# TensorE in source order, with longer attention steps and reordered joints, in a two-layer attention decoder

## The chip, the core and the metric

The kernel runs on one NeuronCore of a Trainium2 chip. The metric is device time in microseconds, the median of several executions. The engines work side by side, each through its own list of instructions in order: TensorE (PE; its weight loads appear as PEld), VectorE (DVE), ScalarE (ACT), GpSimd (POOL) and SyncE (SP), which issues the transfers. An instruction waits on semaphores for those of other engines.

## The reference

Two decoder layers on 256 tokens of 1024 numbers, all in float32. Layer A is differential attention: 8 heads, each with two q/k maps of 64 and values of 128. Layer B takes one shared K/V of the residual stream and three groups of dilated windows, 16 heads of 64 for each, whose outputs are mixed by their softmax denominators. Each layer ends with an output projection and a squared-ReLU MLP of width 4096, both added to the residual stream.

```python
# layer A
h = rms_norm(x, a_norm)
q, k, v = split(h @ w_qkv)                      # q, k normalized per 64, gained, rotated
p = softmax(mask(q @ k.T / 8))                  # two maps a head
a = p[:, :, 0] - lam * p[:, :, 1]
x = x + (rms_norm(a @ v, sub_gain) * (1 - lam_init)) @ w_o
x = x + square(relu(rms_norm(x) @ w_up)) @ w_down
# layer B
k, v = split(rms_norm(x, kv_norm) @ kv_w)       # k normalized and rotated, 3 groups
q = rms_norm(x, b_norm) @ w_q                   # the same
o = sum over groups of softmax(lse) * attention(q_g, k_g, v_g)
x = x + o @ w_o
x = x + square(relu(rms_norm(x) @ w_up)) @ w_down
```

## The kernel before

Precision comes from pairs of reduced-precision parts: each weight chunk is split into a high part (`whi`, ScalarE, L82) and a remainder (`wlo`, VectorE, L83), activations likewise, and a product takes three matmuls (L292 to L294, L402 to L404, L488 to L490) or two (L435, L437). `Weights` fetches chunks of up to 128 x 2048 on SP's queue in the order of the list that `plan` made, three chunks ahead, and splits them by halves, at most five halves being alive; a half is given back by `release` after its last matmul.

Layer A: for each of 8 heads one gemm of 384 columns (q, k and values of the head) over 8 k-tiles and two token blocks, in four quarters of 12 matmuls (`gemm`, `gemm_half`). Out of its PSUM banks come the values (L675, L676) and, by `qk_rows`, the normalized and rotated q and k: a square on ScalarE, table product, sum and mean on VectorE, then three instructions on GpSimd (L328 rotation sum, L332 power -1/2, L334 scaling).
The attention of a head is a generator, `attn_A`: transposes of q and k and their split (`qk_T`, L357 and L340/L341); scores (L350), masked maxima (`masked`, L369), their scaled negative `nm` (L538), exponentials (L541), the combination of the two maps (L545 to L550); transposes of the probabilities and split (L554, L558); the product with the values (L565, L566) and normalization (L569 to L580); transposes into the projection's input `oTh`/`oTl` (L584 to L591).
`tick` is called after each quarter (in the projection after each token block, 6 matmuls). It lets the weights split up to two halves, and every live generator come one step nearer to its next part: `yield n` means that the next part follows n ticks later. `WAIT_A` and `WAIT_B` hold these numbers. `start` enters a generator, `finish` ticks until it is done.

Layer B: 8 pairs of heads, each with three gemms of 384 columns, q, k and values, 12 quarters together; `attn_B` starts after the values' gemm. It makes three q/k transposes (a group each), scores and masked maxima of query block 0, then of block 1, then the softmax of both (L612 to L623), then for each head of the pair the transposes of the probabilities (L632) and the product with the values (L646) with its addition (L649 to L651) and the split into `oTh`/`oTl` (L652).

`OutProj` runs over 8 k-tiles: six by `body` while the last generators finish, the last two by `group`, one of four (token block, half of the columns) at a time. `Mlp.run` runs over 16 chunks, up product of chunk j before down product of chunk j-1; the last two down products are left to `Mlp.group`. `boundary` closes a projection or MLP: groups and residual additions (L421, L519), transposes of the new x by halves (`make_hT`, L260, L268, L271), and the first products of the next stage (`first`).

PSUM has 8 banks, shared by all accumulators and transposes (tag `bank`). The q/k row tiles have 6 buffers, the values' tiles 3, softmax tiles 2.

The order in which each engine gets its instructions is set, in this kernel, by the tile framework's scheduler: it goes through the program with a cost model and takes on each engine, of the instructions that are ready by the model, the one that is earliest in the source. `high_priority` moves some splits ahead. This holds for TensorE too.

## Time and profile before

| | |
|---|---|
| Median of 3 runs | 801.36 us (800.72 to 801.68) |
| Profiled execution | 801.55 us, its span 799.5 us |
| Instructions | 11766 |
| PE, matmul | 772.1 us busy (97%), 4408 |
| PEld, weight loads | 686.7 us (86%) |
| DVE | 581.1 us (73%), 985 |
| ACT | 467.0 us (58%), 851 |
| POOL | 190.9 us (24%), 191 |
| DMA | 131.12 MB, mean 164 GB/s |
| Granted TensorE clock | 0.995 of full speed in the mean |

The span runs from the first to the last instruction, times in the rows are counted from its start. Layer A's heads run up to about 101 us, its projection to 137, the first MLP to 314, layer B's pairs to 577, their projection to 617, and the second MLP to the end. In the middle of layer A a head takes 12.1 us. Matmuls are pipelined and their modelled ends overlap, so what a matmul takes of TensorE's time is the distance of two starts, and idle time shows where the pipe ran dry. In a list of instructions, the bracket behind one is the engine's idle time before it and what ended it.

### The profile page before, as it was taken

The page shows a single profiled execution, that of the slowest core. Times are in us where ns is not written, and L with a number is a line of the kernel's source. Part 1 is how long each engine was busy: PE and PEld are TensorE (multiplying, and loading weights), DVE is VectorE, ACT ScalarE, POOL GpSimd, SP SyncE. Part 2 cuts the span into 40 slices and gives each one's busy share as a digit, 9 for nine tenths or more (in the row PEclk, how much of TensorE's full clock was granted, in tenths as well). Part 3 has the DMA queues.
Part 4 walks back from the last instruction along what each step waited for, and adds up shares of the span by engine and source line. Part 5 has one row for each costly group of instructions (what it writes and reads, how often), then busy time and mean ns, then how long its engine had stood idle before and what let it go on. Part 6 is the DMA issues. An engine that isn't in the chain of part 4 may idle for free.

```text
span 799.5 us, 11766 instructions
## 1 busy us (share of the span) xinstructions
PE 772.1 (97%) x4408; PEld 686.7 (86%) x4408; DVE 581.1 (73%) x985; ACT 467.0 (58%) x851; POOL 190.9 (24%) x191
## 2 busy tenths in 40 slices
PE   6999989999999999999999999999997999999998
PEld 6898967888888888999999999999886888888886
DVE  3998987666656666998888888888767666556663
ACT  5667777544444445657586674857766544444441
POOL 2553531300000000555336354363611000000000
PEclk9999999999999999999999999999999999999999
DMA  8643445445555542554443434434442455545531
GB/s 300 229 143 123 158 155 164 169 171 197 198 176 207 171 184 90 187 198 154 136 153 113 157 121 157 158 119 172 159 158 106 158 186 182 210 170 199 187 130 52
DMA packets 22328, 131.12 MB, mean 164 GB/s; under 512 B 2560, under 2 KB 3328, under 8 KB 13056
## 3 DMA queue, kind: packets, MB, share of 16 engines
q1 hardware_dynamic: 22272, 130.38, 46.0%
q8 instruction: 34, 0.56, 0.3%
q14 instruction: 22, 0.18, 0.1%
HBM read 129.32 MB, written 1.05 MB: 163 GB/s over the span
## 4 chain that ended last, share of the span: by engine, by line
PE 64%; DVE 17%; ACT 12%; issue 3%; POOL 2%; DMA 1%; SPq 0%; POOLq 0%; DVEq 0%; ACTq 0%
PE wps L435 15%; PE wps L437 7%; PE acc L488 7%; PE acc L489 7%; PE acc L490 7%; DVE wlo L83 5%; PE acc L292 4%; PE acc L294 4%; PE acc L293 4%; ACT whi L82 4%; ACT sm L618 2%; DVE sm L369 2%; PE wps L632 2%; DVE T L317 2%; ACT smA L541 2%
## 5 line engine op out<-in xcount | busy, mean ns | idle before, releaser
L83 DVE TENSOR_TENSOR wlo<-raw,whi 128x1024 fp32r<-128x1024 f32 (+1 forms) x272 | 307.0, 1138 | 153.9 <-ACT whi L82 153.7
L82 ACT ACTIVATE whi<-raw 128x1024 fp32r<-128x1024 f32 (+1 forms) x272 | 258.9, 957 | 211.1 <-issue 74.9
L435 PE MATMUL wps<-hT,whi 128*128 128x512 f32 x512 | 182.2, 399 | 2.0 <-DVE hT L271 2.0
L437 PE MATMUL wps<-hT,wlo 128*128 128x256 f32 x512 | 142.9, 280 | 0.0
L435 PEld LDWEIGHTS wps<-hT,whi 128*128 128x128 f32 x512 | 95.9, 188 | 26.0 <-DVE hT L271 3.2
L328 POOL TENSOR_TENSOR T<-T 128x384 f32<-128x384 f32 (+1 forms) x48 | 44.4, 924 | 280.5 <-DVE ms L243 181.6
L488 PE MATMUL acc<-whi,u 128*128 128x512 f32 x256 | 100.4, 392 | 0.3 <-ACT u L340 0.3
L489 PE MATMUL acc<-wlo,u 128*128 128x512 f32 x256 | 100.0, 391 | 0.0
L490 PE MATMUL acc<-whi,u 128*128 128x512 f32 x256 | 98.9, 389 | 0.0
L437 PEld LDWEIGHTS wps<-hT,wlo 128*128 128x128 f32 x512 | 96.6, 189 | 1.4
L292 PE MATMUL acc<-whi,hT 128*128 128x384 f32 x256 | 88.8, 349 | 0.3 <-ACT whi L82 0.2
L292 PE MATMUL acc<-whi,hK 128*128 128x384 f32 x256 | 87.6, 343 | 0.0
L293 PE MATMUL acc<-wlo,hT 128*128 128x384 f32 x256 | 86.3, 337 | 1.1 <-DVE wlo L83 1.1
L294 PE MATMUL acc<-whi,hT 128*128 128x384 f32 x256 | 86.2, 337 | 0.0
L294 PE MATMUL acc<-whi,hK 128*128 128x384 f32 x256 | 85.8, 335 | 0.0
L293 PE MATMUL acc<-wlo,hK 128*128 128x384 f32 x256 | 85.7, 335 | 0.0
L332 POOL TENSOR_TENSOR f<-ms,half 128x6 f32<-128x6 f32 (+1 forms) x48 | 68.2, 1422 | 4.6 <-DVE ms L323 3.1
L488 PEld LDWEIGHTS acc<-whi,u 128*128 128x128 f32 x256 | 48.1, 188 | 11.7 <-ACT u L340 1.2
L490 PEld LDWEIGHTS acc<-whi,u 128*128 128x128 f32 x256 | 48.1, 188 | 10.6 <-DVE u L341 0.4
L489 PEld LDWEIGHTS acc<-wlo,u 128*128 128x128 f32 x256 | 48.1, 188 | 8.8
L293 PEld LDWEIGHTS acc<-wlo,hT 128*128 128x128 f32 x256 | 48.6, 190 | 1.4 <-DVE wlo L83 1.4
L292 PEld LDWEIGHTS acc<-whi,hT 128*128 128x128 f32 x256 | 48.6, 190 | 1.4 <-ACT whi L82 0.5
(117 smaller groups left out, 1204.9 us busy)
## 6 DMA issues: line engine op xcount, KB each, us to landing
raw<-in_wB SPq DMA_DIRECT2D x48, 768.0 KB, 4.2
raw<-in_wup SPq DMA_DIRECT2D x32, 1024.0 KB, 4.8
raw<-in_wdn SPq DMA_DIRECT2D x32, 1024.0 KB, 4.8
raw<-in_wA SPq DMA_DIRECT2D x15, 768.0 KB, 4.3
raw<-in_woA SPq DMA_DIRECT2D x4, 1024.0 KB, 4.8
raw<-in_woB SPq DMA_DIRECT2D x4, 1024.0 KB, 4.8
early<-in_x SPq DMA_DIRECT2D x2, 512.0 KB, 5.3
x<-in_xp SPq DMA_DIRECT2D x1, 1024.0 KB, 7.5
```

The lines of the kernel that those rows point to most:

```text
L82: self.nc.scalar.activation(hi[:, :n], raw, AF.Copy)
L83: self.nc.vector.tensor_tensor(lo[:, :n], raw, hi[:, :n].bitcast(F32), op=ALU.subtract)
L292: nc.tensor.matmul(ps, h[:, kt, 0, tok], wh[:, c], start=kt == 0, stop=False)
L293: nc.tensor.matmul(ps, h[:, kt, 0, tok], wl[:, c], start=False, stop=False)
L294: nc.tensor.matmul(ps, h[:, kt, 1, tok], wh[:, c], start=False, stop=kt == KT - 1)
L328: nc.gpsimd.tensor_tensor(u[:, :n].rearrange("p (h a d) -> p h a d", a=2, d=HD // 2), T[:, 0, :n].rearrange("p (h a d) -> p h a d", a=2, d ...
L332: nc.gpsimd.tensor_tensor(f[:, :nsub], ms[:, :nsub], half[:, :nsub], op=ALU.pow)
L435: nc.tensor.matmul(o, wh[:, c], self.h[:, kt].rearrange("p l s -> p (l s)"), start=kt == 0, stop=False, skip_group_check=True)
L437: nc.tensor.matmul(o[:, 0:S], wl[:, c], self.h[:, kt, 0, :], start=False, stop=kt == KT - 1, skip_group_check=True)
L488: nc.tensor.matmul(ps, uh[:, tok], dh[:, c], start=first, stop=False)
L489: nc.tensor.matmul(ps, uh[:, tok], dl[:, c], start=False, stop=False)
L490: nc.tensor.matmul(ps, ul[:, tok], dh[:, c], start=False, stop=last)
```

## The change

- TensorE's instructions run in the order of the source; the other engines keep the scheduler.
- The numbers of ticks become (3, 2, 4, 3, 4) in layer A and (4, 2, 2, 5, 3, 3) in layer B, and the last head of A waits three more at its start.
- `masked` gives the scaled negative maximum itself, as a minimum of scaled scores; `nm` is not computed any more, and the exponentials take the scale -1.
- In layer A `cf`'s second half is a square on ScalarE, the mean's factor is in the squares, and the addition `ms` is on GpSimd.
- In layer B each query block has its softmax right behind its scores. A generator starts after k; the order of the gemms is q, k, values for six pairs, then q, k, q, k, values, values.
- The last two heads of layer A: one gemm of 512 columns for q and k of both, in ticks of half a quarter, then one of 256 for the values of both.
- `boundary` ticks after three groups, makes x's first half right behind them, and runs `first` by quarters with the second half's transposes after the first of them. The MLP leaves only its last down product to the groups.

```diff
-WAIT_A = (2, 2, 4, 2, 3)
-WAIT_B = (2, 2, 2, 2, 2, 3)
+WAIT_A = (3, 2, 4, 3, 4)
+WAIT_B = (4, 2, 2, 5, 3, 3)
+PAIRS = [(hp, i) for hp in range(HP - 2) for i in range(3)]
+PAIRS += [(HP - 2 + e, i) for e, i in ((0, 0), (0, 1), (1, 0), (1, 1), (0, 2), (1, 2))]
...
-    def gemm_half(pss, h, key, j, i, n):
+    def gemm_half(pss, h, key, j, i, n, nk=2):
         for t in range(NT):
+            if t and n != 384:
+                tick()
...
+        for g in range(KT // nk):
+            gemm_half(pss, h, key, g // 2, g % 2, n, nk)
+            if g < KT // nk - 1:
+                tick()
...
-        f = small.tile([P, 8], F32, name="f", tag="f")
+        f = small.tile([P, 16], F32, name="f", tag="f")
...
-    def masked(out, ps, m, init, mx):
-        nc.vector.tensor_tensor_reduce(out, ps, m, 1.0, init, ALU.add, ALU.max, mx)
+    def masked(out, ps, m, nm):
+        nc.vector.tensor_tensor_reduce(out, ps, m, -(HD ** -0.5), 3e38, ALU.add, ALU.min, nm)
...
     def boundary(group, add, outs, ssx, first):
-        for t in range(NT):
-            group(t, 0)
-            add(t, 0)
+        for t, n in ((0, 0), (1, 0), (0, 1)):
+            group(t, n)
+            add(t, n)
             tick()
-        group(0, 1)
-        add(0, 1)
         make_hT(x, 0, outs)
         square_sums(ssx, x, 0)
         group(1, 1)
         add(1, 1)
-        first(0)
+        first(0, 0)
         make_hT(x, 1, outs)
         square_sums(ssx, x, 1)
-        first(1)
+        for i, f in ((0, 1), (1, 0), (1, 1)):
+            first(i, f)
...
             for j in range(1, NFC):
                 nu = self.up(j)
-                if j == NFC - 1:
-                    self.tail = [u, nu]
-                    return
...
         def group(self, t, n):
-            for i in range(2):
-                for f in range(2):
-                    self.down_mm(NFC - 2 + i, self.tail[i], f, t, n)
+            for f in range(2):
+                self.down_mm(NFC - 1, self.u, f, t, n)
...
     def attn_A(hd, qr, kr, vt, oh, ol):
-        yield WAIT_A[0]
+        yield WAIT_A[0] + 3 * (hd == KT - 1)
...
-        nc.vector.tensor_scalar(nm, mx, -(HD ** -0.5), None, op0=ALU.mult)
...
-        nc.vector.scalar_tensor_tensor(cf[:, :, 1], den[:, :, 0], EPS, den[:, :, 0], op0=ALU.mult, op1=ALU.mult)
+        nc.scalar.activation(cf[:, :, 1], den[:, :, 0], AF.Square, scale=EPS ** 0.5)
...
-        nc.vector.scalar_tensor_tensor(ms[:, :2], oss, 1.0 / P, cf[:, :, 1], op0=ALU.mult, op1=ALU.add)
+        nc.gpsimd.tensor_tensor(ms[:, :2], oss, cf[:, :, 1], op=ALU.add)
...
     # attn_B, for each query block b, behind its scores
+            for hh in range(2):
+                nc.scalar.activation(sms[hh][:, b, :], sms[hh][:, b, :], AF.Exp, bias=nm[:, hh:hh + 1],
+                                     scale=-1.0, accum_out=den[:, hh:hh + 1])
+            nc.vector.reciprocal(rd, den)
+            for hh in range(2):
+                nc.scalar.activation(sms[hh][:, b, :], sms[hh][:, b, :], AF.Copy, scale=rd[:, hh:hh + 1])
+            yield WAIT_B[2 + b]
...
-    for hd in range(KT):
+    for hd in range(KT - 2):
...
+    pss = gemm(h, ("Aqk",), 512)
+    vt2 = [values_tile() for _ in range(2)]
+    for e in range(2):
+        qns = rows_A(pss, e * 4 * HD)
+        gens.append(start(attn_A(KT - 2 + e, qns, qns, vt2[e], oh, ol)))
+    tick()
+    pss = gemm(h, ("Av",), 256, 4)
+    for e in range(2):
+        values_A(pss, e * P, vt2[e])
+    tick()
...
+    for hp, i in PAIRS:
+        pss = acc0 if hp == 0 and i == 0 else gemm(hx, ("B", hp, i), 384)
...
+        if i == 1:
+            gens.append(start(attn_B(hp, *[[rows[hp, e, t] for t in range(NT)] for e in range(2)], vts[hp],
+                                     oh, ol)))
...
-    with tile.TileContext(nc) as tc:
+    with tile.TileContext(nc) as tc, tc.manual_schedule(engines={mybir.EngineType.PE}):
```

## Rows read from the trace of the kernel before

**Rows 1.** Windows by stage: length, busy us (instructions) by engine, clock, DMA share, GB/s
```profile
60.41:101.50 41.09, 38.22 (x253) 36.24 (x251) 37.35 (x106) 30.75 (x93) 17.38 (x22) 1.00 0.43 151
101.50:137.10 35.60, 31.51 (x161) 24.03 (x161) 28.51 (x73) 26.71 (x76) 7.70 (x10) 0.95 0.40 137
...
577.00:616.70 39.70, 35.68 (x202) 28.79 (x201) 27.56 (x45) 26.73 (x47) 4.87 (x5) 0.96 0.41 148
```

**Rows 2.** Waits of PE: releaser, total us, times, longest us
```profile
PE wps L350 <- DVE tl L341: 4.1, 4, 1.9
PE wps L632 <- ACT sm L623: 3.9, 6, 1.0
...
PE wps L435 <- DVE hT L271: 2.0, 2, 1.5
```

**Rows 3.** Timeline of one head of layer A: start us, us, engine, line
```profile
73.14 0.60 PE L357 MATMUL wps<-ident,qn 128*128 128x128 f32 x4
...
73.84 0.51 ACT L541 ACTIVATE smA<-smA,nm 128x256 f32<-128x256 f32 x1 [2.67 <-DVE nm L538]
...
77.11 0.58 ACT L340 ACTIVATE th<-wps 128x512 fp32r<-128x512 f32 x1
...
79.19 0.38 PE L350 MATMUL wps<-th,tl 64*128 64x256 f32 x2 [0.96 <-DVE tl L341]
```

**Rows 4.** Groups of VectorE by shape, two heads: busy us, mean ns, idle before
```profile
L538 DVE TENSOR_SCALAR nm<-mx 128x4 f32<-128x4 f32 x2 | 0.7, 366 | 0.0
...
L576 DVE SCALAR_TENSOR_TENSOR ms<-oss,cf 128x2 f32<-128x2 f32 x2 | 0.3, 148 | 0.0
```

**Rows 5.** Timeline of one pair of layer B, ScalarE and TensorE
```profile
466.55 0.72 ACT L618 ACTIVATE sm<-sm,nm 128x512 f32<-128x512 f32 x1 [1.83 <-DVE nm L616]
...
470.92 0.33 PE L293 MATMUL acc<-wlo,hK 128*128 128x384 f32 x1
471.09 0.34 PE L294 MATMUL acc<-whi,hK 128*128 128x384 f32 x1
471.99 0.33 PE L632 MATMUL wps<-ident,sm 128*128 128x128 f32 x1 [0.56 <-ACT sm L623]
```

**Rows 6.** Window with the lower granted clock, columns as in rows 1
```profile
105.90:109.30 3.40, 3.32 (x9) 2.64 (x10) 3.40 (x15) 1.31 (x2) 3.14 (x5) 0.51 0.40 166
```

**Rows 7.** Groups of GpSimd by shape, two heads of layer A
```profile
L332 POOL TENSOR_TENSOR f<-ms,half 128x4 f32<-128x4 f32 x4 | 4.0, 1011 | 0.2
L334 POOL TENSOR_TENSOR qn<-T,f 128x256 f32<-128x256 f32 x5 | 3.8, 770 | 0.4
L328 POOL TENSOR_TENSOR T<-T 128x256 f32<-128x256 f32 x4 | 3.0, 738 | 0.2
L578 POOL TENSOR_TENSOR ors<-ms,half 128x2 f32<-128x2 f32 x2 | 1.4, 696 | 11.9 <-DVE ms L576 11.9
```

**Rows 8.** Timeline of TensorE, the last head's end in layer A
```profile
126.65 0.28 PE L566 MATMUL wps<-v,pA 128*128 128x256 f32 x1
...
129.28 0.39 PE L402 MATMUL acc<-whi,oTh 128*128 128x512 f32 x1
129.50 0.39 PE L403 MATMUL acc<-wlo,oTh 128*128 128x512 f32 x1
130.07 0.33 PE L584 MATMUL wps<-ident,orow 128*128 128x128 f32 x1 [0.18 <-ACT orow L580]
```

**Rows 9.** Timeline of TensorE, the last pair's end in layer B
```profile
606.92 1.22 PE L646 MATMUL wps<-p,v 128*128 128x512 f32 x6 [0.94 <-DVE p L341]
...
610.78 0.53 PE L402 MATMUL acc<-whi,oTh 128*128 128x512 f32 x1 [2.65 <-ACT oTh L340]
```

**Rows 10.** Timeline of a boundary's copies on ScalarE and VectorE, and of a residual addition
```profile
135.73 1.55 ACT L268 ACTIVATE hT<-wps,gcol 128x256 fp32r<-128x256 f32 x4
...
136.59 1.66 DVE L271 SCALAR_TENSOR_TENSOR hT<-wps,gcol,hT 128x256 fp32r<-128x256 f32 x4 [0.21 <-ACT hT L268]
...
795.91 0.75 DVE L519 SCALAR_TENSOR_TENSOR x<-acc,rM,x 128x512 f32<-128x512 f32 x1 [1.97 <-PE acc L490]
```

More of the change, by code (lines that the diff above doesn't have):

```diff
@@ L130, in plan_mlp @@
                 plan(("dn", layer, j - 1), a["wdn"][layer, j - 1], 2 * DM)
-    for hd in range(KT):
+    for hd in range(KT - 2):
         for i in range(2):
             plan(("A", hd, i), a["wA"][hd, i], 4 * 384)
+    for i in range(2):
+        plan(("Aqk", i), a["wAqk"][i], 4 * 512)
+    plan(("Av", 0), a["wAv"], 8 * 256)
     for i in range(4):
@@ L137, in trunk @@
     plan_mlp(0)
-    for hp in range(HP):
-        for i in range(3):
-            for j in range(2):
-                plan(("B", hp, i, j), a["wB"][hp, i, j], 4 * 384)
+    for hp, i in PAIRS:
+        for j in range(2):
+            plan(("B", hp, i, j), a["wB"][hp, i, j], 4 * 384)
     for i in range(4):
@@ L295, in gemm_half, with gemm @@
         W.release(at[(*key, j)], i)
-    def gemm(h, key, n):
+    def gemm(h, key, n, nk=2):
         pss = [accum() for _ in range(NT)]
-        for j in range(2):
-            for i in range(2):
-                gemm_half(pss, h, key, j, i, n)
-                if not (j == 1 and i == 1):
-                    tick()
+        for g in range(KT // nk):
+            gemm_half(pss, h, key, g // 2, g % 2, n, nk)
+            if g < KT // nk - 1:
+                tick()
         return pss
@@ L454, in relu2, with first @@
             return uh, ul
-        def first(self, i):
-            if i == 0:
+        def first(self, i, f):
+            if i == 0 and f == 0:
                 self.ps = [wps(), wps()]
-            for f in range(2):
-                self.up_mm(0, f, range(4 * i, 4 * i + 4))
-                if i == 1:
-                    W.release(at[("up", self.layer, 0)], f)
-                    self.pre(f)
-                tick()
+            self.up_mm(0, f, range(4 * i, 4 * i + 4))
             if i == 1:
+                W.release(at[("up", self.layer, 0)], f)
+                self.pre(f)
+            tick()
+            if i == 1 and f == 1:
                 self.u = self.relu2()
@@ L599, in attn_B @@
         yield WAIT_B[1]
-        mxs = [small.tile([P, 2], F32, name="mx", tag="mx") for _ in range(2)]
         sms = [wk.tile([P, 2, 4 * P], F32, name="sm", tag="sm") for _ in range(2)]
@@ L705, in trunk, with first_B @@
     acc0 = []
-    def first_B(i):
-        if i == 0:
+    def first_B(i, j):
+        if i == 0 and j == 0:
             acc0.extend([accum(), accum()])
-        for j in range(2):
-            gemm_half(acc0, hq, ("B", 0, 0), i, j, 384)
-            if not (i == 1 and j == 1):
-                tick()
+        gemm_half(acc0, hq, ("B", 0, 0), i, j, 384)
+        if not (i == 1 and j == 1):
+            tick()
     boundary(mlp.group, mlp.add, [(3, hq), (2, hk)], ssx, first_B)
@@ L718, in trunk @@
     gens = []
[L719 to L736 removed]
+    rows, vts = {}, [[] for _ in range(HP)]
+    for hp, i in PAIRS:
+        hx = hk if i else hq
+        pss = acc0 if hp == 0 and i == 0 else gemm(hx, ("B", hp, i), 384)
+        for t in range(NT):
+            ps = pss[t]
+            if i < 2:
+                rows[hp, i, t] = qk_rows(ps, 2 * G, rb[NT + t], windows(tabB[:, i, t]))
+            else:
+                vt = wk.tile([P, 2 * G, 2, HD], F32R, name="v", tag="v", bufs=3)
+                psv = ps[:, :384].rearrange("p (g d) -> p g d", d=HD)
+                nc.scalar.activation(vt[:, :, 0, :], psv, AF.Copy, scale=rb[t])
+                nc.vector.scalar_tensor_tensor(vt[:, :, 1, :], psv, rb[t], vt[:, :, 0, :].bitcast(F32),
+                                               op0=ALU.mult, op1=ALU.subtract)
+                vts[hp].append(vt)
+        tick()
+        if i == 1:
+            gens.append(start(attn_B(hp, *[[rows[hp, e, t] for t in range(NT)] for e in range(2)], vts[hp],
+                                     oh, ol)))
     op = OutProj("oB", oh, ol)
```

80 lines of the change are left out of this document (30 added, 50 removed).

## The prediction

> **What bounds the kernel now.** First the busy times by stage. In layer A's heads (60.4 to 101.5 us) TensorE is idle for 41.09 - 38.22 = 2.9 us and VectorE is busy for 37.35 of 41.09; from there to the first MLP TensorE is idle for 4.1 us, and from 577.0 to 616.7, where layer B's last pairs run out, for 4.0 [rows 1]. Second, who ended its stops: the low halves `tl` of the transposed q/k (4.1 us), the softmax `sm` (3.9, in layer B's pairs) and `hT` (2.0) [rows 2]. So TensorE is the bound, only its stops can be won, 2.9 + 4.1 + 4.0 + 3.9 or some 15 us, and in layer A VectorE is close behind it. Third, one such stop. A head's q/k transposes start at 73.14 and end at 73.74; ScalarE copies them only at 77.11, because the exponentials of the head before, which had waited 2.67 us for `nm`, stood in its queue; so the scores start at 79.19, after 0.96 us of idle TensorE [rows 3]. The reader is to see that the distance in steps would do if ScalarE's queue were empty.
>
> The sum goes against the profiled execution's 801.55 us (span 799.5 and 2.05 around it); the median of the runs is 801.36, so 0.2 is taken off at the end.
>
> **Layer A's heads.** `nm` now comes out of the masking instruction (scale -1/8, minimum): 0.37 us a head less on VectorE and in the chain. The square in `cf` goes to ScalarE (0.15 us), and the `ms` addition, also 128x2, to GpSimd [rows 4]. VectorE's share falls from 0.91 [rows 1] to about 0.86 at the same pace (0.67 of the 12 us that a head takes). The first map's exponentials no longer wait for the second map's masks and for a weight split between. The q/k transposes come one step later, which gives GpSimd time. Four stops lie in this stretch, 2.9 us of idle, and each costs about 0.17 more, because the pipe refills (a stop with 0.56 us idle stretched a spacing of 0.17 to 0.90 [rows 5]): 3.5 us. VectorE stays close to full, so I leave a quarter: **-2.7** (bounds: -3.5, all gone; +1, `tl` and `qn` late at more heads).
>
> **From layer A to its projection (101.5 to 137.1).** Of the time here 4.1 us are idle, and in 105.9 to 109.3 the granted clock is at its lower level of 1.2 GHz (0.51 [rows 6]); the stretch's mean of 0.95 makes that 0.05 x 35.6 = 1.8 us [rows 1]. It came after a stop of 1.9 us, the longest by `tl` [rows 2].
> The edit computes q and k of the last two heads first (512 wide), then both values (256 wide). Columns and weight bytes stay; four weight chunks become three, one transfer less on SP's queue, and DMA is 0.40 busy [rows 1], so transfers stay hidden (a late chunk would cost its landing of 4 to 5 us once). What changes is where the chains end. GpSimd gets four row preparations at once, each 1.01 + 0.77 + 0.74 = 2.5 us [rows 7]: 10.1 us, and normalizations of earlier heads between. Until the last head's q/k transposes I count 5.6 us of values, two projection steps of 6 products at 0.22 [rows 8] = 2.7, and some 3.5 of other heads' pieces, 11.8 together: a stop of about 0.8 (0 to 4, the upper end by the 3.4 us that a copy lagged in rows 3).
> The last head's output is late too. Before, its transposes came 130.07 - 126.65 = 3.4 us after the start of the last values product, 3.3 after its end [rows 8], and the scheduler had laid some thirteen projection products into that time. Now the values product comes with the eleventh projection step and the transposes after the twelfth and three empty steps; in source order one step (1.4 us) and another head's two transposes (0.2) lie between: a stop of 1.7, with the addition on GpSimd (0 to 0.70, the power of as many elements [rows 7]) 1.9.
> The `tl` stop falls from 1.9 to 0.6. The 1.5 us before the MLP (most of `hT`'s 2.0 [rows 2]) fall to 0.6: no weight half is released before the last group, so no split stands ahead of the copies there. The half clock goes with its stop; I give a new one, after the 1.9, one chance in two. Sum: 0.8 + 1.9 - 1.3 - 0.9 - 1.8 + 0.9 - 0.5 (small stops by output rows) = **-0.9** (bounds -4 and +7).
>
> **Layer B's pairs.** The repeating stop: the maxima of both blocks come first, ScalarE waits 1.83 us for `nm`, and the probability transposes find `sm` unfinished, 471.09 to 471.99 [rows 5]. Six such stops hold 3.9 us of idle [rows 2], 4.8 with the refill. Now the softmax goes block by block without `nm`, with five steps instead of four between the second block's scores and the transposes: 5 x 12 products at 0.17 = 10.4 us, against two exponentials and two scalings of 0.72 each [rows 5] behind two masks, under 5 us. They go. Starting after k instead of v brings the q/k transposes nearer to k: five steps and the pieces between, 13 us, against two row preparations of 2.5 x 1.5 = 3.8 us each (estimate by rows 7, 384 columns for 256). New is one cluster of 26 pieces behind a pair's first step, which wants 9 of 8 PSUM banks: two of the gemm, one kept by the second value tile, 1 + 2 + 3 of the pieces. The output's bank comes free about when the third transposes want it. I take 0.5 in all: **-4.3** (bounds -5.4 and +2).
> The Trainium skill (Perfetto Trace Analysis, Optimization Strategy) says that a gap that repeats on the engine that should be saturated can mean that SBUF or PSUM is short for the next tile. Here the releaser is ScalarE's work on `sm`, not a freed bank, so the trace does not bear it out; by the rule longer steps, which hold tiles longer, would keep the 4.8.
>
> **The last two pairs.** q and k of both come first, then the values, so pair six ends in the fourth projection step and pair seven in the twelfth, the last; before, four empty steps followed. The values product that waited 0.94 us for `p` [rows 9] has three steps instead of two and does not wait. The last output still needs the 2.65 us up to the projection [rows 9], and only three products of the other tile (0.7) now stand in front: 2.0. Around the first projection step more than eight banks are wanted, and pair seven's second softmax tile waits for pair six's transposes: +0.6. The half clock (0.04 x 39.7 = 1.6 us [rows 1]) follows a shorter stop: I take off 0.7. Together -0.9 - 0.2 (refill) - 0.7 + 0.6 - 0.7 = **-1.9** (bounds -4 and +3).
>
> **Boundaries and the end.** The down products of the last chunk but one now run before the boundary, so the last `u` has 24 products (5.4 us) of cover and costs nothing. But a group has 6 products instead of 12: 1.4 us of cover. Into layer B ScalarE's four copies (1.55 us) and VectorE's four (1.66) come twice, and the last addition (0.75) queues behind VectorE's [rows 10], so the second transposes wait about 0.9: **+0.9** (0 to 2.5, if the copies are late at all three boundaries). The final outputs leave at half the spacing: **+0.1**. The wider `f` tile is off every chain: 0.
>
> Sum: -2.7 - 0.9 - 4.3 - 1.9 + 0.9 + 0.1 = -8.8; 801.55 - 8.8 - 0.2 = 792.6, say **793**.
>
> **Rivals.** *The joint of layer A decides, to the slower side.* In source order nothing passes a late instruction. If the copies' lag of 3.4 us [rows 3] stays and four row preparations meet it, the heads' 2.7 are not won, `qn` costs 4, `tl` 1.9 more than before, the output transposes 1.9 + 2, another half-clock stretch 1.8: +11.6 there, -4.3 - 1.9 + 1.0 elsewhere, 801.4 + 6.4 = 808. It decides once the joint costs over 5.2. For it: VectorE at 0.91 [rows 1]; against: no stop by these tiles is longer than 1.9 now [rows 2].
> *All ends are hidden.* The lighter VectorE runs ahead, and bank waits, boundary and half clock cost nothing: 793 - 0.8 - 1.3 - 0.9 - 0.5 - 0.9 - 0.6 = 788.
> *One layer does not yield.* VectorE is the true bound in layer A, and 2.7 and 1.3 stay; or layer B's gap is one of buffers, and 4.3 stays: 797 either way. The row on `sm` speaks against the second.
>
> **Chances.** Forecast 0.45 (790 to 796), all hidden 0.2 (785 to 790), one layer without yield 0.2 (796 to 800), the joint 0.15 (800 to 808). The range, 786 to 801, leaves out the tails of the second and the last. A difference under 0.2%, 1.6 us, cannot be told from none; below 799.8 lie the first two and most of the third: faster 0.78, same 0.1, slower 0.12.
>
> **What would show it.** Right: no idle ahead of layer B's probability transposes; exponentials in layer A within 1 us of the masks; heads without idle ahead of the scores; one stop of about 2 us ahead of the last output transposes in A, and one ahead of the last projection tile in B. Wrong: heads in A at 12 us as before; idle before the q/k transposes in every pair; over 4 us of idle between layer A's values and its projection's end.

## The result, and the profile after

The changed kernel takes **823.05 us** (median of 4 runs, 820.85 to 823.23) against 801.04 us of the kernel before (median of 4, 800.60 to 801.68): 1.0265 times as long (95% interval 1.0251 to 1.0280). I had forecast 793, faster. The profiled execution took 820.85 us, of which the span is 819.1.

Where the 19.6 us of span went is read by stage, from the starts of TensorE's products: A from layer A's first q/k/v product to the first up product; MLP 1 from there to layer B's first product, boundary included; pairs from there to layer B's first projection product; end from there to the second MLP's first up product; MLP 2 to the last product.

```
us                A      MLP 1   pairs   end    MLP 2   span
before          126.5    180.5   259.3   39.7   178.8   799.5
after           137.6    181.4   270.1   35.9   179.1   819.1
```

Layer A lost 11.1 us and the pairs 10.8; layer B's end won 3.8; MLPs and boundaries lost 1.2. One caution: 30 products of the last pair (12 q/k transposes, 18 score products) now run ahead of the first projection product and ran behind it before. By their spacing before they take 2.4 us, so with equal work the pairs lost 8.4 and the end won 1.4.

Windows, columns as in rows 1, layer A's heads and end, the pairs and layer B's end; and the pairs of the kernel before:

```profile
69.30:109.10 39.80, 33.88 (x201) 29.56 (x198) 29.26 (x81) 26.52 (x83) 19.80 (x24) 0.89 0.29 106
109.10:148.40 39.30, 33.37 (x165) 26.93 (x165) 24.46 (x58) 24.44 (x73) 7.20 (x11) 0.90 0.31 107
329.80:599.90 270.10, 259.34 (x1704) 248.21 (x1703) 217.52 (x364) 175.79 (x312) 130.36 (x109) 1.00 0.41 145
599.90:635.80 35.90, 31.33 (x171) 25.92 (x171) 23.06 (x37) 23.05 (x42) 3.89 (x4) 1.00 0.32 118
```

```profile
317.70:577.00 259.30, 255.30 (x1673) 245.04 (x1672) 216.73 (x372) 173.55 (x306) 126.22 (x109) 1.00 0.44 151
```

In layer A TensorE idles 5.9 us in each window, where [rows 1] had 2.9 and 4.1, and the granted clock averages 0.89 and 0.90. In the pairs the clock is 1.00 and VectorE's busy time is that of before (217.52 against 216.73), so its work is nearly the same, and TensorE's idle time grew from 4.0 to 10.8; a steady pair takes 35.1 us instead of 33.8. At layer B's end the clock is 1.00, where [rows 1] had 0.96. Who ends TensorE's stops now, columns as in rows 2:

```profile
PE wps L357 <- DVE tl L348: 6.3, 8, 1.7
PE wps L586 <- ACT orow L582: 4.5, 2, 2.9
PE wps L643 <- DVE p L348: 4.3, 5, 0.9
PE wps L364 <- DVE ot L647: 4.3, 5, 1.0
PE wps L364 <- POOL qn L341: 3.7, 3, 1.7
PE acc L409 <- ACT oTh L347: 2.7, 1, 2.7
PE wps L357 <- DVE ot L647: 1.8, 1, 1.8
PE wps L357 <- DVE v L674: 1.1, 1, 1.1
PE acc L496 <- DVE u L348: 0.8, 1, 0.8
PE wps L442 <- DVE hT L277: 0.5, 2, 0.3
```

The probability transposes' stops by `sm` (3.9 us in [rows 2]) are gone, as I said, and `hT` fell from 2.0 to 0.5. In their place stand the values by `p` and the third q/k transposes by `ot` (the copy that frees their PSUM bank), both once in every steady pair. One pair, timelines of ScalarE, VectorE and TensorE:

```profile
450.64 2.31 ACT L86 ACTIVATE whi<-raw 128x768 fp32r<-128x768 f32 x3
452.85 1.08 ACT L347 ACTIVATE p<-wps 128x512 fp32r<-128x512 f32 x2
...
453.56 1.40 DVE L87 TENSOR_TENSOR wlo<-raw,whi 128x768 fp32r<-128x768 f32 x1
454.88 0.22 DVE L330 TENSOR_SCALAR ms<-ss,rB 128x6 f32<-128x6 f32 x1
455.01 1.82 DVE L87 TENSOR_TENSOR wlo<-raw,whi 128x768 fp32r<-128x768 f32 x2
456.75 1.28 DVE L348 TENSOR_TENSOR p<-wps,p 128x512 fp32r<-128x512 f32 x2
...
459.35 2.04 DVE L87 TENSOR_TENSOR wlo<-raw,whi 128x768 fp32r<-128x768 f32 x2
461.31 0.68 DVE L647 TENSOR_TENSOR ot<-wps,ot 64x512 f32<-64x512 f32 x1
...
458.09 1.22 PE L643 MATMUL wps<-p,v 128*128 128x512 f32 x6 [0.85 <-DVE p L348]
...
462.04 0.33 PE L364 MATMUL wps<-ident,qn 128*128 128x128 f32 x1 [0.99 <-DVE ot L647]
```

The reader is to see what stands in front. ScalarE has copied `p` by 453.9, yet VectorE first does three weight splits and takes `p` up only at 456.75; ScalarE's half of `ot` is done at 459.9 and VectorE's follows 1.4 us later, behind two more splits. TensorE does not wait for any of these splits here.

In layer A the longest stop, 2.92 us, is at the fifth head's output (GpSimd, ScalarE, TensorE):

```profile
108.57 1.71 POOL L335 TENSOR_TENSOR T<-T 128x256 f32<-128x256 f32 x1
110.25 1.01 POOL L339 TENSOR_TENSOR f<-ms,half 128x4 f32<-128x4 f32 x1
111.34 1.34 POOL L341 TENSOR_TENSOR qn<-T,f 128x256 f32<-128x256 f32 x1
112.63 0.19 POOL L578 TENSOR_TENSOR ms<-oss,cf 128x2 f32<-128x2 f32 x1
112.90 0.69 POOL L580 TENSOR_TENSOR ors<-ms,half 128x2 f32<-128x2 f32 x1
...
113.63 0.69 ACT L582 ACTIVATE orow<-orow,ors 128x128 f32<-128x128 f32 x2 [2.99 <-POOL ors L580]
...
114.09 0.47 PE L586 MATMUL wps<-ident,orow 128*128 128x128 f32 x1 [2.92 <-ACT orow L582]
```

The squares were summed by 109.3. The addition `ms`, moved to GpSimd, takes 0.19 us, but starts at 112.63, behind a row preparation of the last head; the power `ors`, which was on GpSimd before the change too, comes right behind it.

### The profile page after: what moved, and what is told of

Its sections match the earlier page's. It is cut to its first block, busy times and chain, and to the rows that moved or that the text cites. A ratio compares the mean times of both kernels' runs of the same rounds, so it can differ in the third digit from the quotient of the medians.

```text
span 819.1 us, 11730 instructions
## 1 busy us (share of the span) xinstructions
PE 777.3 (95%) x4408; PEld 691.6 (84%) x4408; DVE 576.8 (70%) x943; ACT 468.4 (57%) x857; POOL 203.5 (25%) x199
## 4 chain that ended last, share of the span: by engine, by line
PE 53%; DVE 19%; ACT 11%; POOL 9%; issue 6%; DMA 1%; SPq 0%; POOLq 0%; DVEq 0%; ACTq 0%
PE wps L442 14%; DVE wlo L87 8%; PE acc L496 7%; PE acc L495 7%; PE acc L494 7%; PE wps L444 7%; POOL f L339 3%; ACT whi L86 3%; ACT sm L615 3%; DVE T L324 3%; POOL T L335 2%; POOL qn L341 2%; PE acc L409 2%; ACT smA L542 1%; DVE ss L328 1%
## 5 line engine op out<-in xcount | busy, mean ns | idle before, releaser
L335 POOL TENSOR_TENSOR T<-T 128x384 f32<-128x384 f32 (+1 forms) x48 | 50.9, 1061 | 315.5 <-DVE ms L249 177.9
L300 PE MATMUL acc<-whi,hT 128*128 128x384 f32 (+2 forms) x256 | 91.0, 355 | 0.0
L301 PE MATMUL acc<-wlo,hT 128*128 128x384 f32 (+2 forms) x256 | 88.2, 345 | 0.0
L302 PE MATMUL acc<-whi,hT 128*128 128x384 f32 (+2 forms) x256 | 88.0, 344 | 0.0
```

The costliest lines, as they stand in the source:

```text
L300: nc.tensor.matmul(ps, h[:, kt, 0, tok], wh[:, c], start=kt == 0, stop=False)
L301: nc.tensor.matmul(ps, h[:, kt, 0, tok], wl[:, c], start=False, stop=False)
L302: nc.tensor.matmul(ps, h[:, kt, 1, tok], wh[:, c], start=False, stop=kt == KT - 1)
L335: nc.gpsimd.tensor_tensor(u[:, :n].rearrange("p (h a d) -> p h a d", a=2, d=HD // 2), T[:, 0, :n].rearrange("p (h a d) -> p h a d", a=2, d ...
```

## The experiments

All are the changed kernel with the edit named, but for the second. I read them by stage, since an edit in one layer leaves the other alone: the pairs' stage is 270.1 to 270.3 in four kernels that have the changed pairs. Layer A's is less sure: unchanged, it took 137.6, 140.1 and 140.1, and 135.5 in e12, where only the tile `f` differs, with different half-clock stretches (stretches with the granted clock at 1.2 GHz, half of 2.4). The moved products of the last pair lie as before in e2, e3 and e14; in e5 and e9 only the 12 transposes (1.2 us) have moved, in all others all 30. The stages are those of the one profiled execution (e1's was its longest, 821.3 us), the median that of all.

```
us                       A      MLP 1   pairs   end    MLP 2   median  ratio to before
e1_scheduler_orders    134.3    181.3   270.1   39.4   179.9   817.08  1.0205 (1.0177, 1.0233)
e2_before_source_order 127.4    185.6   260.7   41.5   181.2   812.78  1.0141 (1.0121, 1.0161)
e3_old_B               140.1    182.9   259.2   41.7   180.7   819.86  1.0225 (1.0208, 1.0242)
e4_old_A               122.9    182.4   270.3   37.5   180.7   812.85  1.0136 (1.0117, 1.0154)
e5_waits               131.4    181.1   286.7   38.7   179.0   834.08  1.0390 (1.0355, 1.0425)
e6_plain_heads         129.8    182.8   288.6   36.3   180.7   833.65  1.0398 (1.0382, 1.0413)
e7_small_ops           134.0    182.9   272.1   38.8   180.7   823.27  1.0263 (1.0246, 1.0281)
e8_p_ahead             128.4    181.4   270.0   38.6   179.0   812.69  1.0137 (1.0119, 1.0156)
e9_p_ahead_old_steps   131.5    183.2   265.0   39.7   180.7   817.79  1.0198 (1.0183, 1.0213)
e10_parts_joined       125.1    182.8   263.5   36.8   180.5   805.86  1.0046 (1.0034, 1.0059)
e11_parts_joined_2     122.7    181.5   266.0   36.3   179.0   801.00  0.9993 (0.9982, 1.0004)
e12_narrow_f           135.5    182.9   270.2   40.4   180.5   826.43  1.0318 (1.0286, 1.0350)
e13_rd_gpsimd          140.1    181.4   273.5   36.3   179.1   826.25  1.0315 (1.0291, 1.0339)
e14_p_ahead_rd         123.2    180.9   262.4   44.0   179.1   806.70  1.0071 (1.0056, 1.0086)
e15_half_the_low_splits 130.5   181.4   255.1   40.1   179.0   801.52  0.9999 (0.9985, 1.0012)
e16_joint_alone        129.0    181.4   266.4   42.0   179.0   814.33  1.0156 (1.0141, 1.0171)
e17_parts_joined_3     123.1    181.4   261.1   47.2   179.0   808.84  1.0088 (1.0071, 1.0104)
```

### Which part: source order, layer A, layer B

**e1_scheduler_orders.** 

> The changed kernel, but TensorE's instructions ordered by the scheduler again. Theory Q (queue order): the changed kernel loses because nothing may pass a product whose input VectorE has late; then the scheduler puts products into these stops, the 10.8 us that layer B's pairs lost and most of the 11 us of layer A come back, and with the 3.8 us won at layer B's end it is at or below the kernel before: 798 to 806. Theory N (new arrangement): the early start of the pairs, the cluster of 26 pieces and the q/k-then-values heads make the pieces late whoever orders TensorE: 816 to 824.

```diff
-    with tile.TileContext(nc) as tc, tc.manual_schedule(engines={mybir.EngineType.PE}):
+    with tile.TileContext(nc) as tc:
```

**e2_before_source_order.** 

> The kernel before, with nothing changed but TensorE in source order. Theory Q: its own late pieces (sm, tl, the output rows) now hold TensorE each time, so it loses most of what the change lost: 812 to 825. Theory N: source order by itself costs little, 799 to 805, and the loss sits in the rest of the change.

```diff
-    with tile.TileContext(nc) as tc:
+    with tile.TileContext(nc) as tc, tc.manual_schedule(engines={mybir.EngineType.PE}):
```

**e3_old_B.** 

> The changed kernel with layer B's attention as before (start after the values, maxima of both blocks first, old steps, pairs in their plain order); source order stays. Theory N: the pairs go back from 35.1 to about 33.8 us, -10.8, and the 3.8 us won at layer B's end are lost: 815 to 818. Theory Q: the old steps find sm unfinished in source order, pairs stay at 35 us or more, and the end is lost as well: 824 to 832.

```diff
-WAIT_B = (4, 2, 2, 5, 3, 3)
+WAIT_B = (2, 2, 2, 2, 2, 3)
...
-        if i == 1:
+        if i == 2:
             gens.append(start(attn_B(...
```

**e4_old_A.** 

> The changed kernel with layer A's heads as before (eight heads of 384 columns, old steps, maximum and nm apart, small ops on VectorE); source order stays. Theory N: the joint's stops by qn (3.7 us) and by the output rows (4.5) and the half-clock stretches behind them go: 811 to 815. Theory Q: in source order the old heads wait for tl and sm instead: 820 to 828.

```diff
-WAIT_A = (3, 2, 4, 3, 4)
+WAIT_A = (2, 2, 4, 2, 3)
...
-    for hd in range(KT - 2):
+    for hd in range(KT):
```

In e3 `attn_B` and in e4 `attn_A` are whole as before. Source order costs 11.6 us in the old kernel, 7.5 of them in the MLP stages, where products now stop up to 2.2 us for `u` at the MLP's end; with the changed boundary that stop is not there. Without source order the changed kernel is 6 us faster, so theory Q holds for a part of the total. It does not explain the pairs: 270.1 whoever orders TensorE, and 259.2 and 260.7 with the old pairs in source order. There theory N holds. Layer A as before, with the changed boundary behind it, takes 122.9 in source order, 14.7 less than changed and less than the 126.5 of before, without a half-clock stretch; in e2, with the old boundary, it takes 127.4 with two. Of the 14.7 us, 7.0 are TensorE's waits (14.0 against 7.0 in e4); the rest is wider spacing of the products, of which the changed kernel's half-clock stretches in layer A, 17.1 us long in all, can make 8.5 at most.

### Which of the edits in each layer

**e5_waits.** 

> The changed kernel with two rows of step counts only. Layer A: the old ones (2, 2, 4, 2, 3). Layer B: counts that put every piece on the step of the gemm on which it stood before (q/k transposes after the third quarter of the next pair's q, probabilities and values as before), while the softmax block by block stays. Read by stage. Layer B: theory C (the 26 pieces behind one step, which want more PSUM banks than there are, and probabilities that meet the row preparations of k, cost the 10.8 us) gives 257 to 260 us of pairs; theory S (the new order of the softmax puts masks and scalings badly on VectorE and ScalarE) leaves 268 to 271. Layer A: theory W (the longer steps keep tiles and bring transposes and rows together) gives 126 to 130 from the first product to the MLP; theory J (the last two heads as q/k then values cost it) leaves 134 to 140. Total: 802 to 806 with C and W, 811 to 815 with one of them, 820 to 825 with neither.

```diff
-WAIT_A = (3, 2, 4, 3, 4)
-WAIT_B = (4, 2, 2, 5, 3, 3)
+WAIT_A = (2, 2, 4, 2, 3)
+WAIT_B = (6, 2, 2, 4, 2, 3)
```

**e6_plain_heads.** 

> The changed kernel with an edit in each layer. Layer A: all eight heads as plain heads of 384 columns; its new steps and small operations stay. Theory J: 123 to 128 us from the first product to the MLP; theory W: 134 to 138. Layer B: the old softmax (both maxima first, nm apart) on the new steps, with the start after k and the cluster of 26 pieces. Theory C: the pairs stay at 268 to 272; theory S: 258 to 261. Total: 811 to 815 with J and C, 800 to 804 with J and S, 820 and more with W and C.

```diff
-WAIT_B = (4, 2, 2, 5, 3, 3)
+WAIT_B = (4, 2, 2, 2, 3, 3)
...
+            nm = small.tile([P, 2], F32, name="nm", tag="nm")
+            nc.vector.tensor_scalar(nm, mxs[hh], -(HD ** -0.5), None, op0=ALU.mult)
...
-    for hd in range(KT - 2):
+    for hd in range(KT):
```

**e7_small_ops.** 

> The changed kernel with an edit in each layer. Layer A: nm, the square in cf and the ms addition back on VectorE with the maximum, as before; steps and the last two heads stay new. If the ms addition behind GpSimd's row preparations is what holds the output rows (2.9 + 1.5 us and a half-clock stretch), layer A falls from 137.6 to about 131; if the order of the last two heads or the steps hold it anyway, 135 to 139. Layer B: the q/k transposes one step later, everything else of the pairs on its new step, so that values and transposes no longer want the banks at one step. If banks alone stop the pairs, the 1.0 us a pair before the third transposes goes and the pairs take 260 to 263; if it is VectorE's order, p stays late (0.85 a pair) and new stops take the place of the old: 266 to 271.

```diff
-WAIT_B = (4, 2, 2, 5, 3, 3)
+WAIT_B = (5, 2, 2, 4, 3, 3)
...
-        nc.gpsimd.tensor_tensor(ms[:, :2], oss, cf[:, :, 1], op=ALU.add)
+        nc.vector.scalar_tensor_tensor(ms[:, :2], oss, 1.0 / P, cf[:, :, 1], op0=ALU.mult, op1=ALU.add)
```

Both theories for layer B fell. The new softmax on the old steps takes 286.7 us, the old softmax on the new steps 288.6, each far worse than both together. In layer A e5 (131.4) and e6 (129.8) fall between the ranges of their theories. For layer B e5 shows why; ScalarE, VectorE and TensorE of one pair:

```profile
449.88 3.04 ACT L86 ACTIVATE whi<-raw 128x768 fp32r<-128x768 f32 x4
452.82 1.07 ACT L347 ACTIVATE p<-wps 128x512 fp32r<-128x512 f32 x2
...
453.38 3.50 DVE L87 TENSOR_TENSOR wlo<-raw,whi 128x768 fp32r<-128x768 f32 x3
456.80 1.28 DVE L348 TENSOR_TENSOR p<-wps,p 128x512 fp32r<-128x512 f32 x2
...
448.83 1.04 PE L629 MATMUL wps<-ident,sm 128*128 128x128 f32 x8
...
458.13 2.08 PE L643 MATMUL wps<-p,v 128*128 128x512 f32 x6 [3.14 <-DVE p L348]
```

TensorE had the probabilities transposed at 449.87. ScalarE does four weight splits before it copies them and VectorE three more; the products wait 3.14 us. In e6 TensorE's waits in the pairs are for `ot` (8.4 us) and `wlo` (7.6) above all. I took it that each edit gave another order of the splits among the pieces on the two engines, and that this order decides; e9 tests it. In e7 the bank stop went, `p` stayed at 0.9, and `sm` (0.6 us a pair) and 0.35 by `wlo` came: 272.1.

In layer A e7 has `nm`, the square and `ms` on VectorE again and takes 134.0, between its ranges. If the moved `ms` held the output rows, their stops had to shrink from 4.5 us; they grew, and `ors` still starts 1.2 us after VectorE is done with `ms` (108.6), behind a row preparation on GpSimd:

```profile
PE wps L590 <- ACT orow L586: 5.5, 2, 3.7
```

```profile
109.22 0.61 POOL L341 TENSOR_TENSOR qn<-T,f 128x256 f32<-128x256 f32 x1
109.79 1.68 POOL L584 TENSOR_TENSOR ors<-ms,half 128x2 f32<-128x2 f32 x1
```

### Theory V: weight splits ahead of the pieces

**e8_p_ahead.** 

> The changed kernel, steps of layer B as changed. Layer B: no weight half is split in the two steps ahead of a pair's first probabilities, and the splits that come later in the program are queued on ScalarE and VectorE behind the probabilities' copies and the output's; nothing else. Theory V (weight splits queued ahead of the pieces that TensorE waits for): VectorE's p comes some 3 us earlier, the 0.85 us stop a pair goes, and the output's copy, which stood behind two splits, comes earlier too, so that the 1.0 us stop at the bank shrinks: 255 to 261 us of pairs. Theory C (the cluster and its banks): p is not late any more, but the third q/k transposes still wait for the bank: 264 to 268. Layer A: eight plain heads with the old steps, but the small operations as changed (nm from the masking instruction, square on ScalarE, ms addition on GpSimd): the term of -2.7 by itself. If it holds, 119 to 121 us from the first product to the MLP, against 122.9 with the old operations; if GpSimd's ms addition holds the output rows, 125 and more. Total: 793 to 800 with V and the term, 806 to 812 with neither.

**e9_p_ahead_old_steps.** 

> Layer B: the step counts of the run that had 286.7 us of pairs (every piece on its step of before, softmax block by block), with the same edit: no splits in the two steps ahead of the first probabilities, and later ones queued behind the copies of probabilities and outputs. Theory V: the values' waits of up to 3.2 us for p go, and the pairs fall by over 20 us, to 256 to 264. If the softmax by block itself is what costs (VectorE stands 1 us at each rd for the exponentials), they stay above 275. Layer A: eight plain heads with the old small operations and the new, longer steps: the steps alone. 122 to 125 us if the steps cost nothing in themselves, 128 to 132 if they do.

```diff
     def pump(self):
+        if self.hold > 0:
+            self.hold -= 1
+            return
...
-                    split(p2[:, b, :, 0], ...
+                    W.behind = split(p2[:, b, :, 0], ...
...
+            for ins in self.behind:
+                st.enter_context(self.tc.issue_after(ins))
             self.nc.scalar.activation(hi[:, :n], raw, AF.Copy)
```

In e9 the pairs fall by 21.7 us, from e5's 286.7 to 265.0, with nothing changed in layer B but when and where the splits are queued. TensorE's idle time in the pairs falls from 19.9 us to 7.7, and e5's half-clock stretches there, 23.9 us long, are gone. Its longest waits in the pairs, e5 and then e9:

```profile
PE wps L643 <- DVE p L348: 16.8, 6, 3.2
PE acc L301 <- DVE wlo L87: 3.1, 5, 0.7
```

```profile
PE acc L309 <- DVE wlo L92: 4.6, 7, 0.8
PE wps L643 <- ACT sm L632: 2.7, 1, 2.7
```

In e8 the `p` stop goes too, but a weight half comes 1.0 us late instead and the bank stop stays: 270.0, against the expectation. Order alone is not enough there.

**e13_rd_gpsimd.** 

> The changed kernel with the reciprocal rd of layer B on GpSimd (as a power of -1) instead of VectorE; the orders of all other instructions stay. VectorE stands some 1.0 us at rd twice a pair, waiting for two exponentials. If these waits are what makes p and the output's copy late, both stops (0.85 and 1.0 us a pair) shrink and the pairs take 258 to 263 us; if VectorE only waits there for what would stop it at the next weight split anyway, 268 to 271.

```diff
-            nc.vector.reciprocal(rd, den)
+            nc.gpsimd.tensor_tensor(rd, den, minus1, op=ALU.pow)
```

Both stops of a pair stay (0.9 and 1.0 us; pairs 273.5, above both ranges): VectorE's standing at `rd` is not the cause.

**e15_half_the_low_splits.** 

> The changed kernel, but in the q/k/v weights of both layers the low half is computed for every other half chunk only; the other one uses its neighbour's (this leaves out part of the computation). That takes six of twelve splits of 0.93 us a pair off VectorE, on no other engine. Theory V (VectorE has no slack, and what stands in its queue ahead of p, ot and tl makes them late): all stops of layer B's pairs go, 254 to 258 us, and in layer A the stops by tl and orow shrink: 126 to 131. Theory C (the third q/k transposes want a PSUM bank that the arrangement itself does not leave free): their 1.0 us a pair stays, 262 to 265. For layer A, if GpSimd's chain (row preparations, then the ms addition) is what holds the joint, qn 3.7 and orow 4.5 us stay and it takes 133 to 137.

```diff
+        short = i == 1 and c in self.short
+        lo = self.parts[c, 0][1] if short else \
+            self.pool.tile([P, WSLOT // 2], F32R, name="wlo", tag="wlo", bufs=self.halves)
...
+        if not short:
             self.nc.vector.tensor_tensor(lo[:, :n], raw, hi[:, :n].bitcast(F32), op=ALU.subtract)
```

**e16_joint_alone.** 

> Layer A: the last two heads as q/k then values, with the steps and the small operations of before (the term priced at -0.9, alone), f 8 wide. With the old heads layer A took 122.9 to 125.1 us; if the term was right, 122 to 124; if the joint costs by itself what the three parts together cost, 133 or more. Layer B: the steps as changed, but the second head's probability transposes one step later, which takes two of the nine PSUM banks off the crowded step. If nine wanted of eight banks make the 1.0 us stop before the third transposes, it goes, and the pairs take 262 to 264 us; if VectorE only moves its lateness, p and tl take its place: 267 to 271.

```diff
+            if hh == 1:
+                yield 1
             p2 = wk.tile([P, 2, 4, 2, P], F32R, name="p2", tag="p2")
...
-            yield WAIT_B[4 + hh]
+            yield WAIT_B[4 + hh] - hh
```

With half of VectorE's weight splits for the pairs gone, they take 255.1 us, less than before the change, and up to the last two pairs the trace names no wait of TensorE at all, none at a bank either. A window of e15, columns as in rows 1:

```profile
360.00:560.00 200.00, 200.00 (x1352) 194.33 (x1351) 138.51 (x249) 139.36 (x244) 104.34 (x92) 1.00 0.43 145
```

The arrangement therefore leaves banks enough if VectorE is in time. With two banks fewer wanted (e16) the bank stop falls from 1.0 to 0.15 us a pair, `p` stays at 0.9, and the pairs take 266.4, between the two ranges. e16's waits up to the last two pairs:

```profile
PE wps L649 <- DVE p L348: 4.4, 5, 0.9
PE wps L364 <- POOL qn L341: 0.9, 2, 0.7
```

So VectorE's lateness makes both stops, and nine wanted of eight banks turn one piece's lateness into the second. Layer A falls by 7.1 us to 130.5 in e15; its waits there:

```profile
PE wps L590 <- ACT orow L586: 6.0, 2, 4.4
PE wps L368 <- POOL qn L345: 3.0, 2, 1.7
PE wps L361 <- DVE tl L352: 1.3, 3, 0.6
```

`tl` falls from 5.1 us (six stops, layer A's share of the 6.3 above) to 1.3, and one half-clock stretch of the four is left, so VectorE's load is a part of layer A's loss too. `orow` and `qn`, GpSimd's chain, stay: the joint's stops are not VectorE's. The three parts of layer A, each alone with the other two as before (122.7 to 125.1 in the five runs with all three old): small operations 128.4 (e8), longer steps 131.5 (e9), joint 129.0 (e16). Each costs: against e4 5.5, 8.6 and 6.1 us, together more than the 14.7 of all three. Half-clock stretches, of which e4 has none there, are in these numbers (10.2, 10.2 and 6.8 us long).

### Can the parts be joined?

**e10_parts_joined.** 

> TensorE in source order with the parts that cost nothing by stage: layer A as before; layer B's first six pairs as before (start after the values, old softmax, old steps); of the change the reordered boundaries and MLP ends, and the last two pairs (q and k of both, then the values, start after k with the new steps). If the stages add up as read so far: 122.9 + 182 + 259.2 + 36.5 + 180 us and 11 ahead, span 791.6, time 793 to 796, faster than both. If source order needs the change's longer steps at the end, layer B's end stays at 41 and it comes to 798 to 801.

**e11_parts_joined_2.** 

> The joined parts again (layer A and layer B's first six pairs as before, changed boundaries and MLP ends, TensorE in source order, the last two pairs reordered), with two edits: the sixth pair's q/k transposes one step later than in the run before it, off the step on which the fifth pair's values stand, and the tile f 8 wide as before, not 16. If the 4 us that the pairs lost there came from pieces meeting at one step, the pairs fall from 263.5 to 260 us or less; if from the start after k, they stay. In the runs so far the MLPs' down products took 227 ns in kernels with either a 16-wide f or the mx tile, and 231 with both: if it is the place of the buffers behind them, the second MLP takes 179.0 us here instead of 180.5. Both: 800 to 802; neither: 805 to 807.

**e17_parts_joined_3.** 

> The joined parts that came to 801.0, with the scores of the last two pairs later behind their q/k transposes (two steps more for the sixth pair, one for the seventh). There 2.0 us of idle by tl and two half-clock stretches (6.8 us) behind it were what the pairs lost against the kernel before. If the distance is what tl lacks: pairs and end 299 instead of 302.3 us, total 796 to 799. If VectorE's queue at the seam of the two orders holds tl or p in any case: 800 to 803.

**e14_p_ahead_rd.** 

> Layer B with the softmax block by block on the steps of before, pairs in their plain order, rd on GpSimd, probabilities queued ahead of weight splits as in the run with 265.0 us but with one step held free of splits instead of two; layer A as before, f 8 wide, boundaries and source order as changed. In the run with 265.0 the steady pairs took 34.1 us with one stop of 0.78 at a weight half that had come late. Theory V: with one step that stop goes, and the pairs come to 33.0 to 33.4 us each, 256 to 259 in all, less than the 259.3 of before; the end is the old one, 40 to 42. Total 794 to 800. If the splits' total on VectorE is the limit, p or the weights stay late and the pairs take 262 to 267: 803 to 808.

Of e10's edit, in part:

```diff
+WAIT_B = (2, 2, 2, 2, 2, 3, 2)
+WAIT_E = (4, 2, 2, 2, 3, 3, 3)
...
-        if i == 1:
+        if i == (2 if hp < HP - 2 else 1):
```

Of the others, e11 gives the sixth pair a first wait of 5 and e17 (5, 4, ...) and (4, 3, ...); e14 has the pairs in plain order on e5's steps, e9's edit with one step held and e13's. None beats the kernel before; e10 (805.9) and e17 (808.8) lie above both of their ranges. e11 comes level (0.9993), though its pairs did not fall: layer A wins 3.8 us and the end 3.4, and the pairs lose 6.7 (with equal work 1.0 and 4.3), at the seam between the two orders of pairs, where a `tl` stop of 2.0 us has 6.8 us at half clock behind it. e17 moved that loss into the end. e14's pairs still wait 0.6 us for `p` and 0.5 for a weight half each.

**e12_narrow_f.** 

> The changed kernel with one number changed: the tile f, of which at most 6 elements are used, 8 wide instead of 16, which moves every buffer behind the pool of small tiles by 128 bytes. My prediction priced the wider f at 0. If that holds, nothing moves: 822 to 824, down products at 227 ns. If the place of the buffers sets their rate, they take 231 ns, each MLP 1.5 to 2 us more: 825 to 828.

```diff
-        f = small.tile([P, 16], F32, name="f", tag="f")
+        f = small.tile([P, 8], F32, name="f", tag="f")
```

826.43 against 823.05 us. First and last product of the second MLP, changed kernel and then e12:

```profile
635.81 0.39 PE L442 MATMUL wps<-hT,whi 128*128 128x512 f32 x1
...
814.95 0.39 PE L496 MATMUL acc<-whi,u 128*128 128x512 f32 x1
```

```profile
639.49 0.39 PE L442 MATMUL wps<-hT,whi 128*128 128x512 f32 x1
...
820.01 0.40 PE L496 MATMUL acc<-whi,u 128*128 128x512 f32 x1
```

179.14 against 180.52 us, with one wait of 0.3 us for `hT` in each. The starts of successive down products lie 227 ns apart in the one and 232 in the other (medians). The first MLP's stage is longer by 1.4 us as well; layer A and layer B's end differ with their half-clock stretches (10.2 us of them at the end in e12, none in the changed kernel).

## Why the prediction was wrong

**The step that failed first is the term for layer B's pairs**, -4.3 forecast, +10.8 measured (8.4 with equal work). Its first half held: the `sm` stops went, and `qn` at the earlier start costs 0.7 once. The 0.5 us for the 26-piece cluster failed: it is 1.0 us in every steady pair, and `p` adds 0.85. I compared ten microseconds of steps (60 products at 0.17 are 10.2, not 10.4) with the softmax's own work, "under 5 us", as if ScalarE and VectorE had nothing else. Each pair has twelve weight splits of 0.95 us and more on VectorE, 12 of 35 us, and none was in my sum. Shown by e9 (order, -21.7 from e5), e15 (load, -15.0) and e16 (bank, -3.7). My own example of a late copy [rows 3] had such splits in it. I put its lag down to the exponentials, but they end at 75.7, and then a split stands in front of ScalarE's copy (77.11) and another in front of VectorE's `tl` (78.46):

```profile
75.87 0.83 ACT L82 ACTIVATE whi<-raw 128x768 fp32r<-128x768 f32 x1
...
77.59 0.95 DVE L83 TENSOR_TENSOR wlo<-raw,whi 128x768 fp32r<-128x768 f32 x1
```

The rule that I named from the Trainium skill (Perfetto Trace Analysis, Optimization Strategy), that a repeating gap can mean PSUM too short for the next tile, I set aside for the kernel before, by its releaser. The changed kernel has such a gap at the bank, and e16 bears the rule out for it; e15 shows the same gap gone with as many banks wanted.

**Layer A's heads**, -2.7 forecast: failed in its reason. VectorE's lighter load was to take the stops away; `tl` holds layer A's scores six times for 5.1 us, instead of four times for 4.1. The small operations alone cost 3 to 6 us (e8), the steps alone 6 to 9 (e9), against the five runs with all three parts old.

**The joint**, -0.9 forecast, failed by a place and by terms that were missing. `qn` costs 3.0 us, at the seventh head's transposes; I had priced 0.8, at the last head's, which do not wait. The last head's output stops TensorE for 1.5 us (I took 1.9), but the fifth head's for 2.9, where I had let the small stops by output rows go (-0.5). The GpSimd rows above show its normalization behind the four row preparations, which I had counted only against the last head's transposes. That the preparations' queue causes both stops is read from the trace; no edit tested it by itself. The moved `ms`, which comes 3 us late there, is not the cause (e7). I had priced one half-clock stretch at even chances; two, 10.2 us long, lie at these stops, and two more, 6.8 us, behind stops in the heads (`v` 1.1 us, `tl` 1.7).

Together layer A lost 11.1 us; the rival of the joint had worked out 11.6 for it. It was right in place. Its price came out by luck: against before, `qn` and `tl` cost 2.4 and 1.0 more where it had 4 and 1.9, the output rows 4.0 as it said, and wider spacing, the half clock in it, 3.7 where it had 1.8. It missed the total because it too took layer B's -4.3 as won.

**Right:** `hT` (2.0 to 0.5, where I had most of it fall), and that the `sm` stops and the wait for `p` at layer B's end go. **Right in the number alone:** The last pairs, -1.9 forecast, -3.8 measured, -1.4 with equal work: the last output's stop is 2.7, not 2.0, and the stop at a bank 1.8, not 0.6, but no half-clock stretch follows, where one did before. The boundaries, +0.9 forecast: the first MLP with its boundary takes 0.9 longer, but the second transposes into layer B do not wait. What came is a stop of 0.8 for `u` at the first down products (0.3 before), and one of 0.3 for `hT` that falls into this stage now. **The wider f** at 0 was right only because it was widened: without the `mx` tile it keeps the buffers behind it in place, and narrow it costs 1.4 us in each MLP stage (e12).

**The range** failed for one reason: no case let layer B's pairs lose. Three of the four took their gain as won, and the one without yield put it at nothing at worst; the term's own bound was +2.

Open: why layer A's longer steps cost 8 us by themselves (e9's waits there are spread over `orow` 4.0, `tl` 3.5 and `v` 2.7), and how much of the wider spacing in layer A is the clock's.

## What to carry to other kernels

Where an engine's order mixes pieces that another engine waits for with bulk work for later, price a moved piece by what stands in front of it in that queue, not by the work of its own chain: here three or four splits of 0.9 us decided. An operation given to an idle-looking engine inherits that engine's queue: 0.19 us of work came 3 us late. Whether that costs anything is another question: with it back on VectorE, the next operation in the same queue was late all the same. And when no case of a forecast lets a large term change sign, that case is the missing rival.

## What the runs showed of the hardware

A shift of all later buffers by 128 bytes (8 floats in each of f's four buffers) changes the spacing of the MLPs' down products (512 columns, fp32r) from 227 to 231 or 232 ns: kernels with exactly one of the 16-wide `f` and the `mx` tile have 227 (twelve traces), with both or neither 231 or 232 (seven). The up products of 512 columns keep their spacing, 236 and 235 ns in the changed kernel and e12. And TensorE's stops can reach further than their length. In these windows, the first behind the stop of 1.3 us (`qn`), the second from the last 0.4 us of the stop of 2.9 us (`orow`) on, in layer A, the granted clock is at 1.2 GHz:

```profile
106.82:110.24 3.42, 3.42 (x16) 3.23 (x15) 3.42 (x9) 2.57 (x8) 3.34 (x4) 0.50 0.00 0
113.65:120.48 6.83, 6.39 (x28) 5.26 (x29) 3.88 (x14) 3.58 (x13) 1.07 (x2) 0.50 0.39 146
```

In the pairs a stop of 1.0 us in each was followed by no such window (clock 1.00 in the row above), those of 3.1 us in e5 by several: the clock's mean from 360 to 560 us is 0.95 there. Length alone does not decide: the stop of 2.7 us at layer B's end was followed by none, that of 1.1 us for `v` in layer A by 3.4 us at 1.2 GHz.
